# A hybrid decoder layer on one core: the second token half of x loaded transposed, its root spread by one product, and other PSUM banks for early turns

## The chip, the cores and the metric

The kernel runs on one core of a Trainium2 chip. The metric is the device time of one execution in microseconds. Before the change it is 1091.62 us, the median of 3 runs (1091.47 to 1091.79).

In the text, TensorE is the matrix engine (PE in the profile; PEld are its weight loads), VectorE is DVE, ScalarE is ACT, GpSimd is POOL, and SyncE (SP) issues most DMAs. "Turn" stands for a transposition on TensorE: a product with the identity matrix, whose result lies in PSUM.

## The reference

x has 1024 tokens (T) of 1024 features (D), in float32. The change lies in the first steps of the layer:

```
mod = silu(c) @ w_ada + b_ada                       # sh1, sc1, g1, sh2, sc2, g2
h = rmsnorm(x, pre_w_mix) * (1 + sc1) + sh1         # rmsnorm: x * rsqrt(mean(x*x) + EPS) * w
proj = h @ w_in                                     # columns: aq, ak, av, hq, hf, hi, hg
attn = sliding-window attention(rope(aq), rope(ak), av), normalised
rec  = gated linear recurrence(hq, hf, hi), normalised, times silu(hg)
x = x + g1 * rmsnorm(concat(attn, rec) @ w_out)
h = rmsnorm(x, pre_w_mlp) * (1 + sc2) + sh2
x = x + g2 * rmsnorm(square(relu(h @ w_up)) @ w_down)
```

Products of the projections and the MLP are made in three parts: each operand is split into a rounded upper part (hi) and a rest (lo), and hi\*hi, hi\*lo and lo\*hi are summed.

## The kernel before

The tokens are two halves (th 0 and 1) of four blocks of 128 (tb 0 to 7), the features eight blocks of 128 (kb 0 to 7). The projection contracts over features, so h is needed with features on the partitions, while x is loaded with tokens on the partitions (`load_x`, line 105; one tile of 128x512 per token block and column half). For each token half the kernel does this:

- `norm_sq` (188) squares the rows of x on ScalarE and sums them (tile jx); `norm_rstd` (199) makes the root of a half, a column of four values for each token partition (VectorE t_x, POOL r_x); `norm_scale` (207) multiplies the rows of x by it.
- `first_T` (215) turns the four 128x128 pieces of one feature block of a token half into one PSUM bank xT.
- `first_evac` (231) makes the block of h from it by `split_evac` (223): ScalarE computes hhi = a\*xT + sh, with a and sh per feature; POOL f = hhi - sh; VectorE hlo = a\*xT - f. hhi and hlo are the two parts of h.
- `first_mm` (394) and `proj3` (510) are the products: pq (queries, 512 columns) and pk (keys and values, 256 columns).

The eight feature blocks of the first half are worked through by a loop (lines 462 to 508): at block kb the engines evacuate xT0 of kb, split the weights of kb+1 (`first_wq` on ScalarE, `first_wql` on VectorE), do the upper parts of the products of the four token blocks (`first_mm` with part 0), turn the next block, and do the lower parts. Into this loop are woven the modulations: `mod_mm` and `mod_fold` at kb 1, and, for the feature blocks 4 to 7, sums over the weight rows on VectorE (`mod_sum`, 309, tile macc) and a turn of the sum at kb 3 and 5 (`mod_turn`, 318, tile pmt). Their results a, sh and ns are what `first_evac` of the next block waits for.

At kb 3 the SP queue gets the loads of x for the second half; at kb 5 and 6 its squares are made, at kb 6 its root, at kb 6 and 7 VectorE scales its rows, and at kb 7 its first two blocks are turned (xT1). Lines 673 to 692 do the rest: `qproj` evacuates pq of the first half, the blocks 2 to 7 of the second half are turned and evacuated, `kvproj` evacuates pk, and the query product of token block 4 (pq4) is done three blocks behind. Then `rope` rotates the queries and keys.

From line 695 on, `filler` gives TensorE work beside attention, in the order of i: queries and keys/values of token blocks 4 to 7 (pq4 pk4 pq5 pk5 ... ), then `values`. The first attention block begins with i = 4, by turning the queries (tile pqT).

What sets the order: the engine handles ACT, DVE, POOL, PE and SP are wrapped by a class `Queue`. Between `pin(True, ...)` (358) and `pin(False, ...)` (693) the instructions of ScalarE, VectorE, POOL and TensorE run in the order of the program text. Outside, the tile framework orders each engine's instructions itself. SP is pinned only for the loads of the second half of x; everything issued later on SP comes behind these.

PSUM has eight banks, in three pools: `pmm` two (`mm_ps`), `pb` five (`tp_ps`), `pa` one (`a_ps`). In the loop pq0 and pq1 hold the two banks of pmm; pq2, pq3 and the two banks of pk hold four of pb. One bank of pb and the one of pa remain for the turns, and a turn waits until the bank's former content has been read. In SBUF the tiles of `hT_` come from a pool of 32 buffers, those of `m_` from one of 16.

Of the kernel before, what the change touches and what calls it, by code (L numbers as in the profile page):

```python
# [47 lines left out]
def hybrid_layer(ctx: ExitStack, tc: tile.TileContext, I, out, dbg=None):  # L48
# [46 lines left out]
    def a_ps(name):  # L95
        return pa.tile([P, 512], F32, tag="aps", name=name)
# [134 lines left out]
    def first_evac(th, kb, pst):  # L231
        hh[kb][th] = (hT_(f"hhi{kb}_{th}", F32R), hT_(f"hlo{kb}_{th}", F32R))
        c = slice(kb, kb + 1)
        split_evac(pst, a1[:, c], sh1[:, c], ns1[:, c], *hh[kb][th], f"f{th}_{kb}")
# [80 lines left out]
            else:  # L315
                DVE.scalar_tensor_tensor(macc1[q], wt, c, macc1[q], ALU.mult, ALU.add)

    def mod_turn(q):
        pst = a_ps(f"pmt{q[0]}")
        for j in range(4):  # L320
            PE.transpose(pst[:, j * P:(j + 1) * P], macc1[q][:, j * P:(j + 1) * P], ident)
        red = small.tile([P, 4], F32, tag="mred", name=f"mred1_{q[0]}")
        DVE.tensor_reduce(red, pst.rearrange("p (j k) -> p j k", j=4), AX.X, ALU.add)
        c = slice(2 * q[0], 2 * q[0] + 2)
        s2 = small.tile([P, 2], F32, tag="m1s", name=f"m1s{q[0]}")
        DVE.tensor_tensor(s2, red[:, 2:4], bT[:, 8 + c.start:8 + c.stop], ALU.add)
        DVE.tensor_tensor(sh1[:, c], red[:, 0:2], bT[:, c], ALU.add)
        DVE.scalar_tensor_tensor(a1[:, c], s2, 1.0, prew1s[:, c], ALU.add, ALU.mult)
        DVE.tensor_scalar(ns1[:, c], sh1[:, c], -1.0, None, ALU.mult)
# [129 lines left out]
        first_mm(0, tb, 1)  # L459

    nextq = {1: (1, 0)}
    for kb in range(1, KB):
        q = nextq.get(kb)
        first_evac(0, kb, xT0[kb])
        if kb + 1 < KB:
            first_wq(kb + 1)
        if kb == 3:
            norm_scale(0, 1, ACT)
            pin(True, SP)
            for hf in range(2):  # L470
                for tb in range(4, TB):
                    load_x(tb, (hf,))
            pin(False, SP)
        if kb == 3:
            mod_sum((2, 0), (7,))
        if kb in (3, 5):
            first_wql(kb + 1)
        for tb in range(3):
            first_mm(kb, tb, 0)
        if q:  # L480
            mod_mm(q)
            mod_copy(q)
        if kb in (3, 5):
            mod_turn((kb // 2 + 1, 0))
        first_mm(kb, 3, 0)
        if kb not in (3, 5) and kb + 1 < KB:
            first_wql(kb + 1)
        if q:
            mod_fold(q)
        if kb in (1, 3, 5):  # L490
            first_kv((kb + 1) // 2, DVE)
        if kb < 5:
            mod_sum(*{1: ((2, 0), (0, 4, 1)), 2: ((2, 0), (5, 2, 6, 3)),
                      3: ((3, 0), (0, 4, 1)), 4: ((3, 0), (5, 2, 6, 3, 7))}[kb])
        if kb + 1 < KB:
            xT0.append(first_T(0, kb + 1, a_ps if kb in (2, 4, 6) else tp_ps))
        if kb in (5, 6):
            for tb in range(4, TB):
                norm_sq(tb, (kb - 5,))
        if kb == 6:  # L500
            norm_rstd(1, 0, 4)
            norm_scale(1, 0, DVE)
        if kb == 7:
            norm_scale(1, 1, DVE)
        if kb == KB - 1:
            xT1 = [first_T(1, 0), first_T(1, 1, a_ps)]
        for tb in range(4):
            first_mm(kb, tb, 1)

# [17 lines left out]
    sinT = cload("sinT", [P, TB, 16], pool=XA)  # L527

    def qproj(tb):
        if tb < 5:  # L530
            pq = pq0[tb]
        else:
            pq = mm_ps(f"pq{tb}")
            proj3(pq, htok(tb), wq)
        q = m_(f"q{tb}")
        if tb in (0, 1):
            DVE.tensor_scalar(q, pq, 0.125, None, ALU.mult)
        else:
            ACT.activation(q, pq, AF.Copy, scale=0.125)
        qn.append(q)  # L540

    def kvproj(tb):
        if tb < 4:
            pk = pk0[tb]
        else:
            pk = mm_ps(f"pk{tb}")
            proj3(pk[:, :256], htok(tb), wkv)
        kv = XA.tile([P, 256], F32, tag="kv", bufs=8, name=f"kv{tb}")
        if tb < 4:
            DVE.tensor_copy(kv, pk[:, :256])  # L550
        else:
            ACT.activation(kv, pk[:, :256], AF.Copy)
        kvn.append(kv)

    def rope(tb, nh, eng=POOL):
# [115 lines left out]
            next(att[tb])  # L671

    att = [attention(tb) for tb in range(TB)]
    for kb in range(2):
        qproj(kb)
        first_evac(1, kb, xT1[kb])
    pq0.append(mm_ps("pq4"))
    for kb in range(2, KB + 3):
        if kb < KB:
            first_evac(1, kb, first_T(1, kb, mm_ps if kb == 2 else tp_ps))  # L680
        if kb == 2:
            qproj(2)
            qproj(3)
        if kb == KB:
            for tb in range(4):
                kvproj(tb)
        if kb > 2:
            proj3(pq0[4], htok(4)[kb - 3:kb - 2], wq[kb - 3:kb - 2], kb == 3, kb == KB + 2)
    for tb in range(4):
        eng = DVE if tb < 2 else POOL  # L690
        rope(tb, 8, eng)
# [1046 lines left out]
def layout(x, c, w_ada, b_ada, pre_w_mix, w_in, attn_sinks, attn_out_w, lb_table,  # L1738
           hg_norm_w, w_out, post_w_mix, pre_w_mlp, w_up, w_down, post_w_mlp):
    A = {}  # L1740
    f = lambda a: np.ascontiguousarray(a)
    cols = lambda v: f(np.asarray(v).reshape(-1, P).T)
    A["x"] = f(np.asarray(x)[0])
    t_cT = cols(np.asarray(c)[0])
    wa = np.asarray(w_ada)[0]
    w1 = wa[:, :2048]
    A["wada1"] = f(w1.reshape(4, 2, P, 2, 4, 256).transpose(3, 4, 0, 2, 1, 5).reshape(2, 4, 4, P, 512))
    A["wada1"][:, 2:] = (w1.reshape(2, 4, P, 2, 4, 256)[:, :, :, :, 2:].transpose(0, 4, 1, 2, 3, 5)
                         .reshape(2, 2, 4, P, 512))
    A["wada1"][:, 0] = (w1.reshape(2, 2, 2, P, 2, 8, P)[:, :, :, :, :, :2].transpose(1, 5, 0, 3, 4, 2, 6)  # L1750
                        .reshape(2, 4, P, 512))
    A["wada"] = f(wa.reshape(KB, P, 6, 2, 512).transpose(2, 3, 0, 1, 4))
    ba = np.asarray(b_ada)[0]
    t_bT = cols(ba)
    A["b_g1"] = f(ba[2048:3072])
    A["b_g2"] = f(ba[5120:6144])
    t_prew1 = cols(np.asarray(pre_w_mix)[0])
    t_prew2 = cols(np.asarray(pre_w_mlp)[0])
    A["postw1"] = f(np.asarray(post_w_mix)[0])
    A["postw2"] = f(np.asarray(post_w_mlp)[0])  # L1760
    wi = np.asarray(w_in)[0]
    perm = [0, 4, 1, 5, 2, 6, 3, 7]
    A["w_q"] = f(wi[:, :512].reshape(D, 8, 64)[:, perm].reshape(KB, P, 512))
    A["w_kv"] = f(wi[:, 512:768].reshape(4, 2, P, 256).transpose(0, 2, 1, 3).reshape(4, P, 512))
    A["w_hv"] = f(wi[:, 1792:2304].reshape(KB, P, 512))
    hd = np.stack([wi[:, 1280:1792], wi[:, 768:1280], wi[:, 2304:2816]])
    A["w_hd"] = f(hd.reshape(3, KB, P, 4, P).transpose(3, 0, 2, 1, 4).reshape(4, 3, P, D))
    sk = np.asarray(attn_sinks)[0]
    order = [0, 1, 4, 5, 2, 3, 6, 7]
    A["sinks"] = f(np.broadcast_to(sk[order], (P, 8)))  # L1770
    A["attw"] = f(np.asarray(attn_out_w)[0].reshape(8, 64)[perm].reshape(4, P).T)
    A["lbt"] = f(np.asarray(lb_table).reshape(2, 4, P).transpose(2, 0, 1))
    A["hgw"] = f(np.asarray(hg_norm_w)[0].reshape(P, 1))
    wo = np.asarray(w_out)[0]
    A["w_o"] = f(np.concatenate([wo[:512].reshape(8, 64, D)[perm].reshape(4, P, D), wo[512:].reshape(4, P, D)]))
    A["w_u"] = f(np.asarray(w_up)[0].reshape(KB, P, 32, P).transpose(2, 1, 0, 3).reshape(32, P, D))
    A["w_dn"] = f(np.asarray(w_down)[0].reshape(32, P, D))
    A["tab"] = f(np.concatenate([np.eye(P, dtype=np.float32), t_cT, t_bT, t_prew1, t_prew2], 1))
    inv = (np.float64(500000.0) ** (-np.arange(0, 16, 2) / 16.0)).astype(np.float32)
    ang = (np.arange(1024, dtype=np.float32)[:, None] * inv[None, :]).astype(np.float64)  # L1780
    co, si = np.cos(ang).astype(np.float32), np.sin(ang).astype(np.float32)
    A["cosT"] = f(np.concatenate([co, co], 1).reshape(TB, P, 16).transpose(1, 0, 2))
    A["sinT"] = f(np.concatenate([-si, si], 1).reshape(TB, P, 16).transpose(1, 0, 2))
    i = np.arange(P)
    A["mle"] = (i[None, :] <= i[:, None]).astype(np.int32)
    A["fle"] = (i[:, None] <= i[None, :]).astype(np.float32)
    si_, ti = i[:, None], i[None, :]
    A["hmask"] = (si_ <= ti).astype(np.int32)
    A["rmask"] = f(np.broadcast_to((np.arange(512) % CH != 0).astype(np.float32), (P, 512)))
    return A  # L1790
# [14 lines left out]
```

## Time and profile before

The profiled execution took 1092.06 us by the clock of the runs, its span from the first to the last instruction is 1090.1 us.

| what | number |
|---|---|
| median of 3 runs | 1091.62 us |
| profiled execution, its span | 1092.06 us, 1090.1 us |
| TensorE busy | 1072.2 us, 98% of the span |
| VectorE, ScalarE, POOL busy | 803.5, 585.2, 374.5 us |
| HBM read, written | 147.51, 55.05 MB |
| granted TensorE clock | 0.997 |

How to read it: a row of the timeline gives start, duration, engine, operation, the tile written, the tiles read, the shape and a count where several instructions are merged; in square brackets stand the idle time of the engine ahead of it and what ended it. A matmul row `128*128 128x512` is a product with a 128x128 stationary and a 128x512 moving operand; products overlap, so the distance between two starts is the time that one takes from the queue, and the duration is longer. Two instructions stand for one product in plain fp32. A row of the stretches gives from:to, its length, the busy time and number of instructions of the engine, the granted clock, the share of the DMA engines and GB/s. A row of the waits gives who waited for whom: us in total, times, the longest. A row of the groups ends with the busy time and the mean duration in ns, then the idle time ahead of the group and who ended it; a row of a tile gives minimum, median and maximum ns. Line numbers in the rows are mostly 39, the line of the wrapper.

### The profile page before, as it was taken

Reading aid. Unit: us, or ns where it says so; the run is one execution under the profiler, and the core shown is the slowest. Engines: PE = TensorE matmul, PEld = TensorE weight load, DVE = VectorE, ACT = ScalarE, POOL = GpSimd, SP = SyncE. Lnnn points to the kernel's source line nnn. Section 1 sums busy time; section 2 is a strip of 40 time slices with the busy share of each in tenths; the row PEclk is TensorE's granted clock in tenths of the full one; section 3 lists DMA queues with packets and bytes.
Section 4 is the critical chain, followed back from the end, with each engine's and each line's share of the span. In section 5 each row is a group of like instructions: output and inputs, shape, how many; then the busy total and the mean of one; then the engine's idle time right before and its main releaser. Section 6 shows DMA issues by size and latency. Waiting matters only on the chain.

```text
span 1090.1 us, 16105 instructions
## 1 busy us (share of the span) xinstructions
PE 1072.2 (98%) x5479; PEld 875.2 (80%) x5479; DVE 803.5 (74%) x1336; ACT 585.2 (54%) x1207; POOL 374.5 (34%) x497
## 2 busy tenths in 40 slices
PE   8999999999999999999999999999999999999996
PEld 6888666788888888888888888888888888888885
DVE  4867768878865564559766767777778788899886
ACT  4535553454554754566655555556575543446435
POOL 1163211143234653432543433344333333320014
PEclk9999999999999999999999999999999999999998
DMA  9702202544310252324577776767999888998638
GB/s 355 268 20 65 91 1 59 167 128 126 115 59 30 88 192 88 135 84 140 187 248 251 230 249 217 242 234 248 296 358 323 270 299 264 327 309 276 198 97 139
DMA packets 101826, 203.63 MB, mean 187 GB/s; under 512 B 13040, under 2 KB 13808, under 8 KB 101744
## 3 DMA queue, kind: packets, MB, share of 16 engines
q1 hardware_dynamic: 86256, 155.04, 42.1%
q0 software_dynamic: 15200, 47.20, 14.7%
q8 instruction: 43, 0.70, 0.3%
q10 hardware_dynamic: 288, 0.36, 0.1%
q14 instruction: 39, 0.32, 0.1%
HBM read 147.51 MB, written 55.05 MB: 186 GB/s over the span
## 4 chain that ended last, share of the span: by engine, by line
PE 87%; DMA 4%; DVE 4%; ACT 2%; POOL 1%; issue 1%; SPq 0%; DVEq 0%; POOLq 0%; ACTq 0%
PE pda L39 16%; PE pua L39 14%; PE pdc L39 8%; PE po L39 8%; PE puc L39 7%; PE pu L39 4%; PE pdb L39 4%; PE pub L39 3%; PE phg L39 3%; PE pv L39 3%; PE phq L39 3%; PE phf L39 3%; PE pq L39 2%; DMA wa<-wada 2%; PE o L39 1%; PE sc L39 1%
## 5 line engine op out<-in xcount | busy, mean ns | idle before, releaser
L39 POOL TENSOR_TENSOR b<-b,b 128x512 f32<-128x512 f32 x64 | 90.7, 1417 | 229.8 <-DMA b<-w_dn 229.4
L39 ACT ACTIVATE dw<-dwr 128x512 fp32r<-128x512 f32 x72 | 45.4, 630 | 52.1 <-DMA dwr<-td 36.5
L39 ACT ACTIVATE s<-s 128x512 f32<-128x512 f32 x84 | 53.0, 631 | 32.4 <-DVE s L39 31.1
L39 DVE TENSOR_TENSOR dw<-dwr,dw 128x512 fp32r<-128x512 f32 x72 | 55.6, 773 | 6.4 <-ACT dw L39 6.3
L39 DVE TENSOR_TENSOR acc<-pda,acc 128x512 f32<-128x512 f32 x68 | 46.7, 686 | 14.0 <-PE pda L39 13.8
L39 POOL DMA_DIRECT2D td<-b x64 | 36.4, 569 | 19.0 <-POOL b L39 19.0
L39 DVE TENSOR_TENSOR wt<-s,wt 128x512 fp32r<-128x512 f32 x42 | 39.4, 939 | 2.6 <-ACT wt L39 2.5
L39 ACT ACTIVATE s<-pua 128x512 f32<-128x512 f32 x28 | 16.7, 597 | 40.5 <-PE pua L39 40.5
L39 POOL TENSOR_TENSOR rrf<-ssf,mhalf 128x1 f32<-128x1 f32 x7 | 7.6, 1080 | 88.0 <-DVE ssf L39 88.0
L39 ACT ACT_TABLE_LOAD x28 | 35.9, 1283 | 1.7 <-PEq L1798 1.2
L39 DVE SCALAR_TENSOR_TENSOR macc<-wada,cs,macc 128x512 f32<-128x512 f32 x42 | 33.7, 803 | 3.6 <-DMA wada<-wada 3.0
L39 POOL DMA_DIRECT2D b<-w_dn x64 | 34.5, 542 | 2.7 <-issue 2.7
L39 POOL TENSOR_TENSOR comb<-comb,rd 128x512 f32<-128x512 f32 x8 | 11.7, 1459 | 63.3 <-DVE rd L39 44.2
L39 PE MATMUL pua<-bt_0h,wt 128*128 128x512 f32 x84 | 32.7, 389 | 0.0
L39 PE MATMUL pua<-bt_1h,wt 128*128 128x512 f32 x84 | 32.7, 389 | 0.0
L39 PE MATMUL pua<-bt_2h,wt 128*128 128x512 f32 x84 | 32.7, 389 | 0.0
L39 PE MATMUL pua<-bt_3h,wt 128*128 128x512 f32 x84 | 32.7, 389 | 0.0
L39 DVE TENSOR_TENSOR wt<-a,wt 128x512 fp32r<-128x512 f32 x42 | 30.7, 732 | 0.9 <-ACT wt L39 0.9
L39 ACT ACTIVATE wt<-s 128x512 fp32r<-128x512 f32 x42 | 26.3, 626 | 8.0 <-DVE s L39 7.8
L39 DVE TENSOR_TENSOR s<-puc,s 128x512 f32<-128x512 f32 x14 | 9.7, 690 | 27.9 <-issue 25.4
L39 DVE TENSOR_TENSOR acc<-pdc,acc 128x512 f32<-128x512 f32 x36 | 24.7, 686 | 6.7 <-PE pdc L39 6.6
L39 PE MATMUL pda<-dw,du_6h 128*128 128x512 f32 x96 | 29.6, 389 | 0.0
(766 smaller groups left out, 3764.8 us busy)
## 6 DMA issues: line engine op xcount, KB each, us to landing
dur<-ud SPq DMA_DIRECT2D x112, 256.0 KB, 4.5
wada<-wada SPq DMA_DIRECT2D x64, 256.0 KB, 3.5
b<-w_dn POOLq DMA_DIRECT2D x64, 256.0 KB, 5.4
td<-b POOLq DMA_DIRECT2D x64, 256.0 KB, 3.4
dwr<-td SPq DMA_DIRECT2D x64, 256.0 KB, 4.9
a<-w_u SPq DMA_DIRECT2D x56, 256.0 KB, 4.5
dwr<-w_dn SPq DMA_DIRECT2D x48, 256.0 KB, 4.3
ud<-s SPq DMA_DIRECT2D x42, 256.0 KB, 3.5
```

Of the source, the lines that this page charges most:

```text
L39: ins = op(*args, **kw)
```

## The change

- The host also lays out the second token half of x transposed (`xT1`, eight blocks of 128x512). At kb 5 and 6 of the loop eight loads bring these into SBUF. The turns of the second half and the scaling of its rows are left out. x itself is still loaded, for its squares.
- The root of the second half is spread over all partitions: `dgx` holds four diagonal matrices with the root's values, and one product with a matrix of ones puts the 512 values on each partition of a bank `rbx`. It stands at the head of kb 7. VectorE multiplies each block of xT1 by rbx in place, the first three at once, the others ahead of the evacuations (at step kb the multiplication of kb+2, then the evacuation of kb+1). `first_evac` then reads SBUF in place of PSUM.
- Of the squares of the second half, six are made at kb 5 and two at kb 6, where they were four and four.
- pq4 and pq5 are done together in the loop over kb, one block behind the evacuation, and pq5 no longer among the fillers.
- `qproj` and `kvproj` of the first half are all on ScalarE; the queries of token blocks 0 and 1 and the four keys/values were on VectorE.
- At kb 3 the last step of `mod_sum` for (2, 0) stands ahead of `first_evac`; `mod_turn` at kb 3 uses a bank of `pb`; the turn of x made at kb 3 uses the bank of `pa`, those at kb 4 and 5 a bank of `pb` (4 was in `pa`). `first_wql` at kb 3 and 5 comes behind `mod_turn`.

```diff
-    def mod_turn(q):
-        pst = a_ps(f"pmt{q[0]}")
+    def mod_turn(q, mk):
+        pst = mk(f"pmt{q[0]}")
...
+    xT1 = []
     for kb in range(1, KB):
         q = nextq.get(kb)
+        if kb == 3:
+            mod_sum((2, 0), (7,))
+        if kb == 7:
+            rbx = tp_ps("rbx")
+            PE.matmul(rbx, lhsT=ones, rhs=dgx.rearrange("p a t -> p (a t)"), start=True, stop=True)
         first_evac(0, kb, xT0[kb])
         if kb + 1 < KB:
             first_wq(kb + 1)
+        else:
+            for j in range(3):
+                DVE.tensor_tensor(xT1[j], xT1[j], rbx, ALU.mult)
+            first_evac(1, 0, xT1[0])
+            first_evac(1, 1, xT1[1])
...
-        if kb == 3:
-            mod_sum((2, 0), (7,))
-        if kb in (3, 5):
-            first_wql(kb + 1)
...
-            mod_turn((kb // 2 + 1, 0))
+            mod_turn((kb // 2 + 1, 0), tp_ps if kb == 3 else a_ps)
         first_mm(kb, 3, 0)
-        if kb not in (3, 5) and kb + 1 < KB:
+        if kb + 1 < KB:
             first_wql(kb + 1)
...
-            xT0.append(first_T(0, kb + 1, a_ps if kb in (2, 4, 6) else tp_ps))
+            xT0.append(first_T(0, kb + 1, a_ps if kb in (2, 3, 6) else tp_ps))
+        for tb, hf in {5: ((4, 0), (5, 0), (6, 0), (7, 0), (4, 1), (5, 1)), 6: ((6, 1), (7, 1))}.get(kb, ()):
+            norm_sq(tb, (hf,))
         if kb in (5, 6):
-            for tb in range(4, TB):
-                norm_sq(tb, (kb - 5,))
+            for j in range(4 * kb - 20, 4 * kb - 16):
+                xT1.append(load_raw(hT_ if j < 6 else m_, f"xT1_{j}", I["xT1"][j]))
         if kb == 6:
             norm_rstd(1, 0, 4)
-            norm_scale(1, 0, DVE)
-        if kb == 7:
-            norm_scale(1, 1, DVE)
-        if kb == KB - 1:
-            xT1 = [first_T(1, 0), first_T(1, 1, a_ps)]
+            dgx = t_("dgx", (P, 4, P))
+            DVE.tensor_tensor(dgx, ident.unsqueeze(1).broadcast_to([P, 4, P]),
+                              rx[1].unsqueeze(2).broadcast_to([P, 4, P]), ALU.mult)
...
-    for kb in range(2):
-        qproj(kb)
-        first_evac(1, kb, xT1[kb])
-    pq0.append(mm_ps("pq4"))
-    for kb in range(2, KB + 3):
-        if kb < KB:
-            first_evac(1, kb, first_T(1, kb, mm_ps if kb == 2 else tp_ps))
-        if kb == 2:
-            qproj(2)
-            qproj(3)
-        if kb == KB:
-            for tb in range(4):
-                kvproj(tb)
-        if kb > 2:
-            proj3(pq0[4], htok(4)[kb - 3:kb - 2], wq[kb - 3:kb - 2], kb == 3, kb == KB + 2)
+    pq0.append(a_ps("pq4"))
+    for kb in range(KB):
+        if 0 < kb < KB - 1:
+            if kb + 2 < KB:
+                DVE.tensor_tensor(xT1[kb + 2], xT1[kb + 2], rbx, ALU.mult)
+            first_evac(1, kb + 1, xT1[kb + 1])
+        (qproj if kb < 4 else kvproj)(kb % 4)
+        if kb == 0:
+            pq0.append(mm_ps("pq5"))
+        for tb in (4, 5):
+            proj3(pq0[tb], htok(tb)[kb:kb + 1], wq[kb:kb + 1], kb == 0, kb == KB - 1)
...
+    A["xT1"] = f(np.asarray(x)[0, 512:].T.reshape(KB, P, 512))
```

Beside these, `qproj` takes pq from the list for tb < 6 (it was tb < 5), and the branches to VectorE in `qproj` and `kvproj` are gone.

More of the change, by code (lines that the diff above doesn't have):

```diff
@@ L529, in qproj @@
     def qproj(tb):
-        if tb < 5:
+        if tb < 6:
             pq = pq0[tb]
@@ L535, in qproj @@
         q = m_(f"q{tb}")
[L536 to L539, printed above, removed]
+        ACT.activation(q, pq, AF.Copy, scale=0.125)
         qn.append(q)
@@ L548, in kvproj @@
         kv = XA.tile([P, 256], F32, tag="kv", bufs=8, name=f"kv{tb}")
[L549 to L552, printed above, removed]
+        ACT.activation(kv, pk[:, :256], AF.Copy)
         kvn.append(kv)
```

## The prediction

> **What bounds the kernel now.** I read the page first: TensorE is busy almost throughout, so only what leaves or enters its queue, or stalls it, can move the end.
>
> ```profile
> span 1090.1 us, 16105 instructions
> PE 1072.2 (98%) x5479; PEld 875.2 (80%) x5479; DVE 803.5 (74%) x1336; ACT 585.2 (54%) x1207; POOL 374.5 (34%) x497
> ```
>
> Then the waits of TensorE, first from 20 to 80 us, where the change lies (its two largest), then from 80 us to the end (seven rows, 3.7 us in sum; the first and the last stand here):
>
> ```profile
> PE pmt L39 <- DVE hlo L39: 1.0, 1, 1.0
> PE pmt L39 <- DVE macc L39: 0.9, 1, 0.9
> ...
> PE rb L39 <- DVE dg L39: 1.6, 4, 0.6
> ...
> PE phg L39 <- ACT f L39: 0.2, 1, 0.2
> ```
>
> Next, TensorE alone by stretches: the upper parts of k block 7 (53.95), their lower parts with the first two second-half turns, the stage with the other six turns and pq4, and pq5:
>
> ```profile
> 53.95:56.74 2.79, 2.79 (x18) 1.00 0.02 6
> 56.74:59.02 2.28, 2.28 (x19) 1.00 0.00 0
> 59.02:68.64 9.62, 9.01 (x51) 1.00 0.00 0
> 71.51:76.97 5.46, 5.46 (x26) 1.00 0.02 5
> ```
>
> The clock column is 1.00 in all. The third row holds only 24 products, as many as the fourth, and lasts 4.2 us longer: that is the room here. A piece of TensorE's timeline shows what a turn costs:
>
> ```profile
> 61.32 0.60 PE L39 MATMUL xT<-c_tab,x 128*128 128x128 f32 x4
> 61.68 0.48 PE L39 MATMUL pq<-wq1h,hhi 128*128 128x512 f32 x1
> 62.00 0.39 PE L39 MATMUL pq<-wq1l,hhi 128*128 128x512 f32 x1
> ...
> 79.85 0.60 PE L39 MATMUL pqT<-c_tab,q 128*128 128x128 f32 x4
> ```
>
> Four turns hold the queue 0.36 us (61.32 to 61.68), and the product behind them starts its successor 0.32 later, where 0.23 is usual (5.46 / 24): 0.45 a block. The last row, the start of attention, is my mark.
>
> **The turns of the second half go.** Two of eight lie in the 2.28 row, back to back: 2 x 0.36 + 0.09 = 0.81, so that row becomes 1.47. The other six cost 6 x 0.45 = 2.7 of the 9.62; 24 products at 0.23 take 5.52, so 9.62 - 2.7 - 5.52 = 1.4 are stalls. Pq4 and pq5 together become 48 x 0.23 = 11.04, against 9.62 + 5.46 = 15.08. If nothing stalls, this saves 0.81 + 4.04 = 4.85 us. Pk4 and pk5 keep their lengths, and the moved pq5 takes no cover from anything: it stood ahead of the mark.
>
> **The spread of the root is new on TensorE.** One fp32 product of 128x512; a like one stands near the end:
>
> ```profile
> 1079.65 1.02 PE L39 MATMUL pdly<-x,c_tab 128*128 128x512 f32 x2
> ```
>
> It is two instructions, 1.02 us to the modelled end. The tail by which an end outlasts the successor's start is 0.39 - 0.23 = 0.16 in the timeline above, so it holds the queue 0.86, and 0.09 more behind it as a turn does: 0.95 us. The low bound is 0.36, a set of turns, the high one 1.11, without the tail. It is all on the path: k block 7's products stand behind it in TensorE's queue, also while it waits for dgx.
>
> **The early turns get other banks.** These rows are the two stalls:
>
> ```profile
> 33.12 0.75 DVE L39 SCALAR_TENSOR_TENSOR macc<-wa,cs,macc 128x512 f32<-128x512 f32 x1
> 34.45 0.74 DVE L39 SCALAR_TENSOR_TENSOR macc<-wa,cs,macc 128x512 f32<-128x512 f32 x1
> 35.34 0.63 PE L39 MATMUL pmt<-c_tab,macc 128*128 128x128 f32 x4 [0.91 <-DVE macc L39]
> 37.07 0.69 DVE L39 TENSOR_TENSOR wkv2l<-wkvr,wkv2h 128x512 fp32r<-128x512 f32 x1
> 38.35 0.40 PE L39 MATMUL pq<-wq4h,hhi 128*128 128x512 f32 x1
> ...
> 44.78 0.75 DVE L39 SCALAR_TENSOR_TENSOR macc<-wa,cs,macc 128x512 f32<-128x512 f32 x1
> 45.45 0.75 DVE L39 SCALAR_TENSOR_TENSOR hlo<-xT,a,f 128x512 fp32r<-128x512 f32 x1
> 46.25 0.66 PE L39 MATMUL pmt<-c_tab,macc 128*128 128x128 f32 x4 [1.00 <-DVE hlo L39]
> ```
>
> In block 3 the last sum now precedes hlo: behind the sum at 33.12 it ends at 33.12 + 2 x 0.75 and a gap, about 34.65, and the turn follows 0.15 later as before (34.45 + 0.74 to 35.34), at 34.80 for 35.34. In block 5 hlo's bank is no longer waited for, but the sum is, and VectorE's work up to it is the same: 44.78 + 0.75 + 0.15 = 45.68 for 46.25. The second wait swallows the first gain: 0.57 us in all. The lower weight part of block 4, put behind the turn's reduction and its small steps, follows these at 37.07 - 0.54 = 36.53 and ends 0.7 later, at 37.2; its product comes at 38.35 - 0.54 + 0.23 = 38.0: nothing, and VectorE is where it was, at 37.2 for 37.07. In block 5 it is alike. Block 5's turn of x, now in the ordinary bank, waits for hlo, done at 46.2; TensorE comes to it 1.2 us after the other turn, at 46.9: nothing.
>
> **Is dgx in time?** TensorE reaches the spread at 53.95 - 0.57 = 53.38.
>
> ```profile
> L39 ACT ACTIVATE jx<-x x8: 618/622/627, 43.5 to 51.2; 128x512 f32<-128x512 f32 x8
> 51.90 0.17 DVE L39 SCALAR_TENSOR_TENSOR t_x<-ssx 128x4 f32<-128x4 f32 x1 [0.78 <-ACT jx L39]
> 52.15 1.01 POOL L39 TENSOR_TENSOR r_x<-t_x,mhalf 128x4 f32<-128x4 f32 x1 [2.41 <-DVE t_x L39]
> 88.96 0.69 DVE L39 TENSOR_TENSOR comb<-comb,rd 128x512 f32<-128x512 f32 x1
> ```
>
> Two squares move to block 5, which frees 1.2 us ahead of the others, and everything is 0.57 earlier. ScalarE alone would allow t_x at 50.1; VectorE's order (hlo and a lower weight part before it) puts it at about 50.4, an estimate. Then the root ends at 51.7, and dgx, priced by the last row, at 52.4. Cover 1.0 us; beyond that it costs one for one.
>
> **The second half's blocks** now need two passes on VectorE. The durations are those of the groups from 57 to 72 us, the multiplication's is that of a sum of a PSUM and an SBUF tile on the page:
>
> ```profile
> L39 ACT ACTIVATE hhi<-xT,sh,a 128x512 fp32r<-128x512 f32 x8 | 5.9, 779 | 6.4 <-PE xT L39 6.4
> L39 DVE SCALAR_TENSOR_TENSOR hlo<-xT,a,f 128x512 fp32r<-128x512 f32 x8 | 5.8, 749 | 3.1 <-POOL f L39 3.1
> L39 POOL TENSOR_SCALAR f<-hhi,ns 128x512 f32<-128x512 f32 x8 | 5.5, 697 | 7.4 <-ACT hhi L39 7.4
> L39 ACT ACTIVATE q<-pq 128x512 f32<-128x512 f32 x3 | 1.7, 595 | 2.2 <-PE pq L39 2.2
> L39 DVE TENSOR_TENSOR s<-puc,s 128x512 f32<-128x512 f32 x14 | 9.7, 690 | 27.9 <-issue 25.4
> ```
>
> A block costs VectorE 0.69 + 0.75 = 1.44, ScalarE 0.78 + 0.60 = 1.38 with the evacuation moved to it, POOL 0.70, and TensorE consumes one in 6 x 0.23 = 1.38. The chain multiplication, hhi, f, hlo is 2.92 (some 3.1 with handoffs), and as written it laps over two blocks (a multiplication stands two hlo ahead): 1.54 a block. The multiplication is bounded by the 0.60 of an evacuation and the 0.75 of hlo; 0.69 has its very kinds of operands. For hhi out of SBUF the neighbours are jx at 0.62 and hhi out of PSUM at 0.78; I keep 0.78. Its start: the spread lands at 54.5, three multiplications to 56.6, hlo of block 0 at 57.45, of block 1 at 58.2, of block 7 at 58.2 + 6 x 1.54 = 67.4. TensorE has block 7's products from 54.33 to 58.59 (2.79 + 1.47), needs the first hlo two products later, at 59.05, and the last at 59.05 + 7 x 1.38 = 68.71. So 1.3 us remain, and VectorE's backlog is off the path. The scalings and evacuations taken from VectorE lay beside TensorE's work and give nothing.
>
> **The eight added loads** (2 MB) follow x in SP's queue:
>
> ```profile
> 34.63 4.69 SPq L39 DMA_DIRECT2D x<-x  x8
> x<-x SPq DMA_DIRECT2D x16, 256.0 KB, 5.0
> ```
>
> Issued at 0.59 each from about 40, or from 45.6 where a buffer is freed by the last sum, they land from 50.6 at the latest for the first and 54.8 for the last; block 0 is wanted at 54.5, block 7 at about 65. Queued behind them are small tables and parts of w_hv, all with readers long after. Nothing; if the first came later than 55.8 (54.5 and the 1.3 us of slack), it would cost one for one.
>
> **The sum.** 4.85 + 0.57 - 0.95 = 4.47 us: attention starts at 75.4. What follows hangs on finished work, not on the clock, and nothing there is changed, so I carry it whole. The profiled execution took 1092.06 us (1.96 beside its span), 0.44 over the median of 1091.62. 1092.06 - 4.47 = 1087.59; less 0.44, **1087.2 us**.
>
> **Rivals.** *B, the blocks pace TensorE.* Hlo's first input moves from PSUM to SBUF, so it reads two SBUF tiles, as macc does. Macc stretches where f runs:
>
> ```profile
> 42.72 0.70 POOL L39 TENSOR_SCALAR f<-hhi,ns 128x512 f32<-128x512 f32 x1 [3.97 <-ACT hhi L39]
> 42.82 1.14 DVE L39 SCALAR_TENSOR_TENSOR macc<-wa,cs,macc 128x512 f32<-128x512 f32 x1
> ```
>
> That is 1.14 against 0.75. If each hlo pays it, a block takes 0.69 + 1.14 = 1.83, block 1's hlo ends 0.4 later than above, and the last at 58.6 + 6 x 1.83 = 69.6, 0.9 late: 1088.1. If each waits a whole f, 0.70 + 0.75 = 1.45, a block takes 2.14 and the last, from 58.9, ends at 58.9 + 12.84 = 71.7, 3.0 late: 1090.2. Against it: f can run under the multiplication, which reads one SBUF tile and one PSUM bank like the present hlo, never stretched. The Trainium skill (SBUF — State Buffer, "Who interferes with whom") says that a VectorE instruction with two SBUF inputs and a GpSimd instruction that reads SBUF exclude each other, the later one blocking until the first is done. By that rule the 2.14 case is the harsh end; the 0.39 of the row agrees in sign and is less than a whole f.
>
> *C, the gain is given back later.* Behind the pinned stretch the tile framework orders instructions anew, by its own estimate of when each is ready. The price is bounded by TensorE's waits behind the mark: doubled, they cost 3.7, 1090.9; halved, they add 1.8. For it: attention's chains (rb on dg) are tight. Against: no load or weight there comes at a fixed time.
>
> *D, slower: a block's four steps do not overlap.* Place: the loop of pq4 and pq5. Price: 3.1 a block, the last hlo at 58.2 + 18.6 = 76.8, 8.1 late: 1087.2 + 8.1 = 1095.3. It eats the gain from 2.5 us a block on, (68.71 + 4.47 - 58.2) / 6. Against: in the groups above eight blocks pass within the 15 us of that view, under 1.9 each, though one block's steps take longer, and the multiplications run ahead.
>
> **How the numbers follow.** The forecast has 0.72, B 0.13, C 0.10, D 0.05. This kernel's measurement can tell about 0.2%, 2.2 us, from no change. Faster: 0.72 and 0.08 of B, 0.80. Same: the rest of B, and C, 0.15. Slower: D, 0.05. The range goes up to 1090.2, the harsh end of B; down to 1085.0: the spread at its low bound (0.59 less) and C the other way round, 1.8 less, make 1084.8. It leaves out C's upper end, D and a corner of the forecast, under 0.2.
>
> **What would show it.** Right: no turns after k block 7, pmt at about 34.8 and 45.7, the spread at 53.4 without a wait and 0.86 long, pq4 and pq5 alternating without gaps from 58.6 to 69.6, attention's first turn at 75.4, the rest shifted alike. Wrong: a wait of the spread for dgx, of pq for hlo or hhi, hlo well above 0.75, or a smaller shift at the end than at the mark.

## The result, and the profile after

The changed kernel takes 1086.6 us (median of 6 runs, 1086.37 to 1087.54) beside 1091.7 us for the kernel before in the same session (1091.39 to 1092.88): ratio 0.9953, 95% interval 0.9942 to 0.9964. It is faster by about 5 us, clear of the interval; 1087.2 was predicted, 1085.0 to 1090.2. The profiled execution took 1086.42 us, 5.64 less than that of before. The head of its page:

```profile
span 1084.6 us, 16059 instructions
PE 1067.8 (98%) x5449; PEld 872.2 (80%) x5449; DVE 798.8 (74%) x1331; ACT 587.6 (54%) x1213; POOL 371.3 (34%) x497
```

TensorE is as full as it was, with 30 instructions and 4.4 us of busy time less. Its waits from 20 to 80 us are now one row; the two sums of that row are what is left of the early turns' stalls:

```profile
PE pmt L39 <- DVE macc L39: 1.3, 2, 1.0
```

TensorE's timeline (start, duration, what, idle time ahead of it) at the places that the prediction named. The first row, block 2's first product, is a point ahead of every edit:

```profile
27.02 0.40 PE L39 MATMUL pq<-wq2h,hhi 128*128 128x512 f32 x1
...
34.30 0.63 PE L39 MATMUL pmt<-c_tab,macc 128*128 128x128 f32 x4 [0.37 <-DVE macc L39]
...
45.19 0.63 PE L39 MATMUL pmt<-c_tab,macc 128*128 128x128 f32 x4 [0.97 <-DVE macc L39]
...
52.85 1.02 PE L39 MATMUL rbx<-dgx,ones 128*128 128x512 f32 x2
...
53.94 0.39 PE L39 MATMUL pq<-wq7l,hhi 128*128 128x512 f32 x1
...
67.94 0.39 PE L39 MATMUL pq<-wq7h,hlo 128*128 128x512 f32 x1
...
74.60 0.60 PE L39 MATMUL pqT<-c_tab,q 128*128 128x128 f32 x4
```

The mark, attention's first turn, went from 79.85 to 74.60: 5.25 us. But the same point ahead of the edits lay elsewhere in the kernel before, and the reason is at the very start, where nothing was edited: there a product that reads x waits for the load of x. First the rows of before, then those of after:

```profile
1.66 4.71 PE L39 MATMUL spare<-spare,ones_r 128*128 128x512 f32 x11 [1.66 <-DVE spare L121]
6.98 0.49 PE L39 MATMUL spare<-x,ones 128*128 128x128 f32 x2 [0.61 <-DMA x<-x]
...
27.52 0.39 PE L39 MATMUL pq<-wq2h,hhi 128*128 128x512 f32 x1
```

```profile
1.65 4.09 PE L39 MATMUL spare<-spare,ones_r 128*128 128x512 f32 x11 [1.65 <-DVE spare L121]
6.46 0.49 PE L39 MATMUL spare<-x,ones 128*128 128x128 f32 x2 [0.71 <-DMA x<-x]
```

The product that reads x started 0.52 us earlier in this execution, and 0.50 us of that were still there at block 2. The eleven spare products ahead of it also took 0.62 us less, but that is not the reason: with the turns kept (below) they took 4.23 us, the product behind them still waited 1.72 us for x, to 7.61, and block 2 began at 28.16. In all fourteen profiles block 2 begins 20.5 to 20.8 us behind the product that reads x; in the twelve experiments this is at 27.15 to 28.24. It is a property of the execution, so I count every mark from its own block 2: 52.33 us before, 47.58 after, **4.75 us gained** where 4.47 was predicted. The stretches (from:to, length, busy time, clock, share of DMA, GB/s) say where. First those of before that the prediction does not show: all of k block 7, then pk4, then pk5:

```profile
53.95:59.02 5.07, 5.07 (x35) 1.00 0.01 3
...
68.64:71.51 2.87, 2.87 (x26) 1.00 0.00 0
...
76.97:79.85 2.88, 2.88 (x26) 1.00 0.29 60
```

Then those of after: the spread with all of k block 7, pq4 and pq5 together, pk4 with pk5:

```profile
52.85:57.90 5.05, 5.05 (x28) 1.00 0.11 41
57.90:68.84 10.94, 10.94 (x50) 1.00 0.00 0
68.84:74.60 5.76, 5.76 (x50) 1.00 0.00 0
```

Up to k block 7, 0.60 us came from the early turns (53.95 - 27.52 against 52.85 - 27.02). In k block 7 the spread took what its two turns gave (5.07, 5.05). The stage with the turns and pq4 and that of pq5 (9.62 + 5.46 = 15.08 before) gave 15.08 - 10.94 = 4.14, and pk4 and pk5 nothing (5.75, 5.76).

Behind the mark nothing was given back: mark to end of span is 1010.25 before and 1010.00 after. TensorE's waits from 80 us on still sum to 3.7 us; the first and the last row:

```profile
PE rb L39 <- DVE dg L39: 1.6, 4, 0.6
...
PE x2T L39 <- DVE h L39: 0.2, 1, 0.2
```

The blocks of the second half, on VectorE: the matrix for the spread, the first three multiplications, and the evacuations of blocks 1 and 7.

```profile
51.37 0.69 DVE L39 TENSOR_TENSOR dgx<-c_tab,r_x 128x512 f32<-128x512 f32 x1 [1.12 <-POOL r_x L39]
53.91 1.88 DVE L39 TENSOR_TENSOR xT<-xT,rbx 128x512 f32<-128x512 f32 x3
...
57.56 0.75 DVE L39 SCALAR_TENSOR_TENSOR hlo<-xT,a,f 128x512 fp32r<-128x512 f32 x1 [0.52 <-POOL f L39]
...
66.80 0.75 DVE L39 SCALAR_TENSOR_TENSOR hlo<-xT,a,f 128x512 fp32r<-128x512 f32 x1 [0.82 <-POOL f L39]
```

From 57.56 to 66.80 six blocks pass, (66.80 - 57.56) / 6 = 1.54 each, the predicted pace. The evacuation at 66.80 ends at 67.55 and its product runs at 67.94: 0.39 us to spare, not the 1.3 predicted. Rows of the tiles f and hlo (minimum, median, maximum ns), and of the groups the one of hhi; the nine are the eight blocks of the second half and, ahead of them, block 7 of the first:

```profile
L39 POOL TENSOR_SCALAR f<-hhi,ns x9: 692/694/1207, 52.5 to 66.1; 128x512 f32<-128x512 f32 x9
L39 DVE SCALAR_TENSOR_TENSOR hlo<-xT,a,f x9: 750/752/769, 53.2 to 66.8; 128x512 fp32r<-128x512 f32 x9
```

```profile
L39 ACT ACTIVATE hhi<-xT,sh,a 128x512 fp32r<-128x512 f32 x9 | 7.2, 810 | 6.0 <-DVE xT L39 3.9 <-PE xT L39 2.1
```

Hlo, whose inputs both lie in SBUF now, takes 0.75 to 0.77 us at every block. One f of the nine was stretched, to 1.21 us. It is the second of this pair on POOL, from 56.32 to 57.53, and so starts beside the first hlo, which runs from 56.27 to 57.04; the hlo of block 1 (57.56, above) waited 0.52 us for it.

```profile
55.55 1.98 POOL L39 TENSOR_SCALAR f<-hhi,ns 128x512 f32<-128x512 f32 x2 [2.34 <-ACT hhi L39]
```

### The profile page after: what moved, and what is told of

It reads as the page before. It is cut to its first block, busy times and chain, and to the rows that moved or that the text cites. A ratio compares the mean times of both kernels' runs of the same rounds, so it can differ in the third digit from the quotient of the medians.

```text
span 1084.6 us, 16059 instructions
## 1 busy us (share of the span) xinstructions
PE 1067.8 (98%) x5449; PEld 872.2 (80%) x5449; DVE 798.8 (74%) x1331; ACT 587.6 (54%) x1213; POOL 371.3 (34%) x497
## 3 DMA queue, kind: packets, MB, share of 16 engines
q0 software_dynamic: 15200, 47.20, 14.4%
## 4 chain that ended last, share of the span: by engine, by line
PE 89%; DVE 4%; DMA 4%; ACT 1%; issue 1%; POOL 1%; SPq 0%; DVEq 0%; ACTq 0%; POOLq 0%
PE pda L39 16%; PE pua L39 14%; PE pdc L39 8%; PE po L39 8%; PE puc L39 7%; PE pu L39 4%; PE pdb L39 4%; PE phg L39 4%; PE pub L39 4%; PE phf L39 3%; PE pv L39 3%; PE phq L39 3%; PE pq L39 3%; DMA wa<-wada 2%; PE o L39 1%; PE pk L39 1%
## 5 line engine op out<-in xcount | busy, mean ns | idle before, releaser
L39 POOL TENSOR_TENSOR b<-b,b 128x512 f32<-128x512 f32 x64 | 87.4, 1365 | 223.4 <-DMA b<-w_dn 223.0
L39 DVE TENSOR_TENSOR wt<-s,wt 128x512 fp32r<-128x512 f32 x42 | 36.1, 859 | 2.6 <-ACT wt L39 2.5
L39 DVE TENSOR_TENSOR wt<-a,wt 128x512 fp32r<-128x512 f32 x42 | 34.5, 823 | 0.9 <-ACT wt L39 0.9
L39 PE MATMUL pda<-dw,du_7h 128*128 128x512 f32 x96 | 29.6, 389 | 0.0
L39 PE MATMUL pdc<-dw,du_3h 128*128 128x512 f32 x96 | 29.6, 389 | 0.0
```

The costliest lines, as they stand in the source:

```text
L39: ins = op(*args, **kw)
```

## The experiments

Starts and marks from TensorE's timeline of each profile; "gain" is the time from block 2 to the mark against the kernel before (52.33). Each ratio is to the kernel before on the same chip (medians 1091.7 to 1092.3 us).

| kernel | median us | ratio, interval | block 2 | mark | between | gain | mark to end |
|---|---|---|---|---|---|---|---|
| before | 1091.7 | | 27.52 | 79.85 | 52.33 | | 1010.25 |
| after | 1086.6 | 0.9953 (0.9942 to 0.9964) | 27.02 | 74.60 | 47.58 | 4.75 | 1010.00 |
| banks only | 1091.47 | 0.9994 (0.9985 to 1.0002) | 27.95 | 79.67 | 51.72 | 0.61 | 1009.83 |
| no other banks | 1087.37 | 0.9960 (0.9946 to 0.9973) | 27.42 | 75.52 | 48.10 | 4.23 | 1009.78 |
| lead lost | 1096.43 | 1.0038 (1.0025 to 1.0051) | 28.24 | 84.80 | 56.56 | -4.23 | 1010.60 |
| turns kept | 1091.53 | 0.9994 (0.9985 to 1.0002) | 28.16 | 79.80 | 51.64 | 0.69 | 1010.30 |
| two spreads | 1088.44 | 0.9968 (0.9956 to 0.9981) | 27.55 | 75.98 | 48.43 | 3.90 | 1011.12 |
| three spreads | 1089.53 | 0.9974 (0.9965 to 0.9983) | 27.66 | 76.98 | 49.32 | 3.01 | 1010.62 |
| squares late | 1091.08 | 0.9988 (0.9979 to 0.9997) | 27.56 | 79.33 | 51.77 | 0.56 | 1010.07 |
| late but busy | 1090.37 | 0.9982 (0.9973 to 0.9991) | 27.15 | 77.53 | 50.38 | 1.95 | 1010.27 |
| squares 4 and 4 | 1087.27 | 0.9956 (0.9943 to 0.9969) | 27.75 | 75.51 | 47.76 | 4.57 | 1009.79 |
| turn later | 1087.42 | 0.9961 (0.9948 to 0.9974) | 28.07 | 75.62 | 47.55 | 4.78 | 1009.98 |
| POOL split | 1086.53 | 0.9947 (0.9935 to 0.9960) | 27.75 | 74.95 | 47.20 | 5.13 | 1009.75 |
| combined | 1086.73 | 0.9951 (0.9938 to 0.9965) | 27.80 | 74.77 | 46.97 | 5.36 | 1009.83 |

My theory is the prediction's: the gain is the second half's turns and the stalls they brought, plus the early banks, less the spread. Its rivals are that the blocks pace TensorE, and that the gain is lost or made behind the mark.

**The banks by themselves, and everything but the banks.** The kernel before with the four edits of k blocks 3 to 5; the changed kernel with these four undone.

```diff
-        pst = a_ps(f"pmt{q[0]}")
+        pst = mk(f"pmt{q[0]}")
...
+        if kb == 3:
+            mod_sum((2, 0), (7,))
         first_evac(0, kb, xT0[kb])
...
-            xT0.append(first_T(0, kb + 1, a_ps if kb in (2, 4, 6) else tp_ps))
+            xT0.append(first_T(0, kb + 1, a_ps if kb in (2, 3, 6) else tp_ps))
```

> The kernel before with the early banks alone: the last sum of block 3 ahead of the evacuation, the other banks of the turns, the lower weight parts behind the turn. Theory (TensorE's queue): the two waits of the modulation turns shrink to about 0.4 and 1.0 us, and since the second is set by VectorE's sums the gain is 0.55 us and not the sum of both: 0.5 to 0.6 us under before, about 1091.1. Rival (each stall counts by itself): 1.9 us under before, 1089.8. Rival (the turns have cover elsewhere): no change.

> The kernel after with the early banks undone. Theory: 0.55 us over after, about 1087.2, and the modulation turns wait 0.9 and 1.0 us as before. Rival (each stall counts): 1.9 over after, 1088.5. Rival (cover elsewhere): as after.

The mark moved by 0.61 us with the banks alone, and without them the changed kernel gained 0.52 less. The two parts add up: 0.61 and 4.23 are 4.84, against 4.75 together. A gain of 0.6 is too small for whole times: with the banks alone the interval includes no change, so this part is shown by the profiles only.

**The multiplications' lead.** In the changed kernel only two blocks are multiplied ahead, and each further one directly before its own evacuation, so that the four steps of a block form one chain.

```diff
-            for j in range(3):
+            for j in range(2):
                 DVE.tensor_tensor(xT1[j], xT1[j], rbx, ALU.mult)
...
-            if kb + 2 < KB:
-                DVE.tensor_tensor(xT1[kb + 2], xT1[kb + 2], rbx, ALU.mult)
+            DVE.tensor_tensor(xT1[kb + 1], xT1[kb + 1], rbx, ALU.mult)
             first_evac(1, kb + 1, xT1[kb + 1])
```

> The kernel after with each multiplication right ahead of its own evacuation from block 2 on (two done at once instead of three). Theory: the four steps of a block then follow one another, 0.67 + 0.78 + 0.91 + 0.72 = 3.08 us from start to start in the profile after; block 1's hlo ends at 58.3, block 7's at 58.3 + 6 x 3.08 = 76.8, where 67.9 is wanted: 8.9 us over after, 1095.5, slower than before, and TensorE waits for hhi and hlo in the stage of pq4 and pq5. Rival (the order of multiplications is a detail, the engines overlap anyhow at about 1.5 us a block): within 0.5 us of after.

The kernel is slower than before. TensorE's waits from 20 to 85 us, and then two of VectorE's evacuations, five blocks apart:

```profile
PE pq L39 <- DVE hlo L39: 4.2, 5, 0.8
PE pq L39 <- ACT hhi L39: 1.5, 5, 0.3
PE pmt L39 <- DVE macc L39: 1.4, 2, 1.0
```

```profile
61.81 0.75 DVE L39 SCALAR_TENSOR_TENSOR hlo<-xT,a,f 128x512 fp32r<-128x512 f32 x1 [1.67 <-POOL f L39]
...
77.22 0.75 DVE L39 SCALAR_TENSOR_TENSOR hlo<-xT,a,f 128x512 fp32r<-128x512 f32 x1 [1.73 <-POOL f L39]
```

A block takes (77.22 - 61.81) / 5 = 3.08 us, and the mark comes 8.98 us later than in the changed kernel. This is the price that rival D had, at its place: the three multiplications ahead of the loop decide the sign of the whole change.

**Pq5 beside pq4, with the turns kept.** The kernel before, with pq5 done in the loop of pq4 (`qproj` takes it from there too).

```diff
-    pq0.append(mm_ps("pq4"))
+    pq0 += [mm_ps("pq4"), a_ps("pq5")]
...
-            proj3(pq0[4], htok(4)[kb - 3:kb - 2], wq[kb - 3:kb - 2], kb == 3, kb == KB + 2)
+            for tb in (4, 5):
+                proj3(pq0[tb], htok(tb)[kb - 3:kb - 2], wq[kb - 3:kb - 2], kb == 3, kb == KB + 2)
```

> The kernel before with pq5 done beside pq4 in the loop over the second half, the turns kept. Theory: six turns of 0.45 stay in the queue and only the stalls of that stage find cover: 11.0 + 2.7 = 13.7 us instead of 9.62 + 5.46 = 15.1, so 1.3 us under before, about 1090.4. Rival (the gain of the change is the evacuations' waits, covered by the second product, and the turns are nearly free): 3.5 to 4.5 us under before, 1087 to 1088.

A miss by half: 0.69 us. The head of that stage on TensorE shows why:

```profile
59.64 0.60 PE L39 MATMUL xT<-c_tab,x 128*128 128x128 f32 x4
60.58 0.63 PE L39 MATMUL xT<-c_tab,x 128*128 128x128 f32 x4 [0.34 <-DVE hlo L39]
61.17 0.47 PE L39 MATMUL pq<-wq0h,hhi 128*128 128x512 f32 x1
```

The second turn starts 0.94 us behind the first instead of 0.36, and a first product follows 0.59 behind that: 0.8 us of the stalls lie ahead of the stage's first product, where no pq5 can cover them. The stage takes 14.40 us here (59.64 to 74.04). So the 4.14 us split into 15.08 - 14.40 = 0.68 for pq5 beside pq4, six turns at the predicted 0.45, 2.7, and some 0.8 of stalls that left only with the turns. The turns' own 2.7 and these 0.8 were not taken out by themselves; that they leave with the turns is read from the two stages.

**The price of the spread.** The product issued two and three times, onto the same bank.

```diff
-            PE.matmul(rbx, lhsT=ones, rhs=dgx.rearrange("p a t -> p (a t)"), start=True, stop=True)
+            for _ in range(2):
+                PE.matmul(rbx, lhsT=ones, rhs=dgx.rearrange("p a t -> p (a t)"), start=True, stop=True)
```

> The kernel after with the spread's product made twice into the same bank; the second writes what the first wrote. Theory: the spread lies whole on TensorE's path, so the second adds its own 0.86 us, and the multiplications behind it start as much later: 0.8 to 0.9 over after. Rival (the spread is hidden in a wait of TensorE for k block 7): no change.

> The spread product is issued three times instead of once. Theory: each added product costs 0.85 us at the mark, and what follows is carried whole: mark 1.7 us later than in the changed kernel, counted from the same start, end 1.7 later, median about 1088.3 to 1088.6. Rival: a later mark costs more behind it, as the run with two spreads seemed to show (0.85 at the mark, 1.6 to 2 at the end): end 3.2 to 4 us later, median 1089.8 to 1090.6, with the time from the mark to the end 1.5 us or more above the changed kernel's 1010.0.

TensorE's timeline of the kernel with two, then of that with three; the second row of each is the second product behind the spread:

```profile
53.37 1.88 PE L39 MATMUL rbx<-dgx,ones 128*128 128x512 f32 x4
...
55.32 0.39 PE L39 MATMUL pq<-wq7l,hhi 128*128 128x512 f32 x1
```

```profile
53.51 2.74 PE L39 MATMUL rbx<-dgx,ones 128*128 128x512 f32 x6
...
56.32 0.40 PE L39 MATMUL pq<-wq7l,hhi 128*128 128x512 f32 x1
```

From the spread to that row it is 1.09, 1.95 and 2.81 us with one, two and three: 0.86 each. (A first product lies in between; its start is drawn into the spread's own span, so the distance to the second is taken.) The marks agree, 0.85 and 1.74 later. But the medians are about 1.8 and 2.9 us above the changed kernel's, more than the marks. In the profiles the excess lies behind the mark, 1.12 us with two and 0.62 with three. It does not grow with the shift, and with three spreads it is less than half of the 1.5 that the rival needed, so the profiles speak against that rival; but the median, 0.9 above the theory's range, lies nearer to the rival's. These medians come from different sessions. Beside the kernel before in the same session, 1091.91 and 1092.3, the two lose 1.6 and 2.3 us of the changed kernel's 5.1, and with intervals of about 1 us to either side this is compatible with the theory's 0.86 and 1.7. With two spreads a part of the excess is a wait that the changed kernel lacks; from 80 us on:

```profile
PE pda L39 <- DVE acc L39: 0.5, 1, 0.5
```

All of TensorE's waits from 80 us on sum to 4.2 us there, to 3.7 in the changed kernel, and to 3.8 with three spreads, where they explain next to nothing. Over all fourteen profiles the time from mark to end lies between 1009.75 and 1011.12 us. The rest of the excess, and whether the spreads bring it, stays open.

**The squares.** All eight at k block 6; then four and four, as before the change; then all late again, with eleven spare products ahead of the spread.

```diff
-        for tb, hf in {5: ((4, 0), (5, 0), (6, 0), (7, 0), (4, 1), (5, 1)), 6: ((6, 1), (7, 1))}.get(kb, ()):
+        for tb, hf in {6: [(tb, hf) for hf in range(2) for tb in range(4, TB)]}.get(kb, ()):
```

> The kernel after with all eight squares of the second half at k block 6. Theory: six squares more stand ahead of the sum, at 0.62 us and less each, so t_x comes at 53.3 instead of 50.1, dgx ends at about 55.2 where TensorE wants it at 52.85: a wait of 2.3 us at the spread, and 2.3 us over after, since TensorE's queue stands behind it in order. Rival (the wait is covered, since the products of k block 7 do not need the spread): within 0.3 us of after.

> The kernel after with four squares at k block 5 and four at 6, as in the kernel before. Theory: t_x moves from 50.1 to about 50.8 and dgx ends at 52.7, just ahead of TensorE at 52.85: no change, the cover of 0.8 us pays for it. Rival (the moved squares are part of the gain): 0.6 to 1.2 us over after.

Four and four cost 0.18 us at the mark: dgx is ready just as TensorE arrives, so moving two squares bought cover and almost no time. All late, the wait was as expected and the mark moved by nearly twice as much, 4.19 us. TensorE's timeline, and its stretches: the wait, the spread, the first and the later products of k block 7, pq4 with pq5, pk4 with pk5 (the fifth number is the granted clock):

```profile
55.93 1.25 PE L39 MATMUL rbx<-dgx,ones 128*128 128x512 f32 x2 [2.38 <-DVE dgx L39]
...
57.40 0.63 PE L39 MATMUL pq<-wq7l,hhi 128*128 128x512 f32 x1
```

```profile
53.55:55.93 2.38, 0.00 (x0) 1.00 0.34 129
55.93:57.40 1.47, 1.47 (x4) 0.78 0.00 0
57.40:59.96 2.56, 2.56 (x9) 0.50 0.00 0
59.96:62.63 2.67, 2.67 (x16) 0.96 0.02 6
62.63:73.57 10.94, 10.94 (x50) 1.00 0.00 0
73.57:79.33 5.76, 5.76 (x50) 1.00 0.00 0
```

Behind a pause of 2.38 us the granted clock is 0.50. The three stretches with less than 1.00 stand for 0.22/0.5 x 1.47 + 2.56 + 0.04/0.5 x 2.67 = 3.4 us at half the clock, which is 1.7 us lost, and the stretch from spread to mark takes 23.40 us instead of 21.75 in the changed kernel. The last two stretches are exactly its own. To tell this from ScalarE's and VectorE's late work, the pause was filled:

```diff
+            for _ in range(11):
+                PE.matmul(rbx, lhsT=ones_r, rhs=wq[0][0], start=True, stop=True)
             PE.matmul(rbx, lhsT=ones, rhs=dgx.rearrange("p a t -> p (a t)"), start=True, stop=True)
```

> As the run with all squares at k block 6, where the spread waited 2.38 us and the mark came 4.19 us after the changed kernel's; ahead of the spread eleven products of 128x512 whose result is overwritten keep TensorE busy while it waits (11 x 0.23 = 2.5 us). In that run the profile shows TensorE's granted clock at 0.50 for 2.6 us behind the wait, and the stretch from the spread to the mark at 23.40 us instead of 21.75. Theory: the 1.65 us are the clock that fell in the pause; with the pause filled the clock stays at 1.00, the stretch is 21.75 again, and the mark is 2.5 to 2.8 us after the changed kernel's, counted from the same start: median about 1089.3 to 1089.8. Rival: the 1.65 us are ScalarE's and VectorE's work that came late; then the stretch stays at 23.4 and the mark 4.2 to 4.4 us late, median 1091.1 to 1091.5.

```profile
53.23 2.66 PE L39 MATMUL rbx<-wq0h,ones_r 128*128 128x512 f32 x11
55.73 1.06 PE L39 MATMUL rbx<-dgx,ones 128*128 128x512 f32 x2
...
77.53 0.60 PE L39 MATMUL pqT<-c_tab,q 128*128 128x128 f32 x4
```

With TensorE kept busy the same late spread reaches the mark in 21.80 us at a clock of 1.00, and the mark is 2.80 us late instead of 4.19, at the edge of what the theory gave (0.24 of it arose already at the second early turn, which waited 1.21 us here); the rival falls. The median, 1090.37, is above the range I gave for it and only 0.7 below that of the unfilled run, and the two intervals overlap. The single executions say why: of the eleven with all squares late, three took 1089.30 to 1089.73 us at a mean clock of 0.997 to 0.998, the other eight 1090.50 to 1092.12 at 0.996, and all eleven of the filled kernel had 0.997 to 0.998. So the same pause seems to have lowered the clock in eight executions and not in three; the profile is of one of the eight, so the clock in the three is inferred from their times.

**What is left at the early turns.** Three tries to take the remaining waits for the sums: both turns one token block later; the lower keys/values weights of k block 3 on POOL instead of VectorE; both, with the squares five and three.

```diff
-            mod_turn((kb // 2 + 1, 0), tp_ps if kb == 3 else a_ps)
         first_mm(kb, 3, 0)
+            mod_turn((kb // 2 + 1, 0), tp_ps if kb == 3 else a_ps)
...
-            first_kv((kb + 1) // 2, DVE)
+            first_kv((kb + 1) // 2, POOL if kb == 3 else DVE)
```

> The kernel after with the modulation turns of blocks 3 and 5 behind the fourth token block's upper part instead of ahead of it. Theory: the turn of block 5 is bound by VectorE's last sum and starts when it did; 0.7 us of products move into its wait; the next bound, the evacuation of block 6 that needs the turned sums, takes back a half: 0.35 us under after. Rival (the wait of 1.0 us is all TensorE's loss): 0.7 to 1.0 us under after. Rival (a later turn delays the next block): slower by up to 0.4 us.

> The lower weight part of the keys/values at k block 3 is made by POOL instead of VectorE. In the changed kernel this VectorE step (0.69 us) lies between the two turned sums, and the last sum of block 5 is waited for 0.97 us. Theory: VectorE reaches the last sum about 0.6 us earlier, the turn of block 5 follows at about 0.5 before its place in the changed kernel (45.19, counted from the same start of the products of block 2), but hhi of the next block is then bound by ScalarE's squares, so the mark moves by 0.3 us to the front: median ratio to the changed kernel 0.9997. Rival 1: POOL's step, which reads two SBUF tiles, holds up VectorE's sums and hlo for about its length: mark 0.5 to 0.8 us later, turn of block 5 later too. Rival 2: the wait only moves from the sum to hlo of block 5: turn earlier, mark within 0.1.

> The step of POOL as in the run beside it, with the squares five at k block 5 and three at k block 6, and both turned sums behind the products of the fourth token block instead of the third. Theory: with ScalarE's squares no longer late, the whole 0.6 us of the wait for the last sum and some of the wait at block 3 come back: mark 0.6 to 0.75 us before the changed kernel's, counted from the same start, and a median near 1086.0. Rival: as the turn alone gave nothing (its sum comes 0.2 us later), only the POOL step's 0.3 shows, or the step's loss.

The later turn alone gained 0.03 us: the wait ahead of the second turn shrinks from 0.97 to 0.35 us, but the turn, on which the next evacuation hangs, starts 0.2 later (18.39 us behind block 2 instead of 18.17). POOL's step gained 0.38, as its theory said, although it takes 1.28 us there for 0.69 on VectorE; its second turn and that step:

```profile
45.55 0.63 PE L39 MATMUL pmt<-c_tab,macc 128*128 128x128 f32 x4 [0.59 <-DVE macc L39]
```

```profile
35.53 1.28 POOL L39 TENSOR_TENSOR wkv2l<-wkvr,wkv2h 128x512 fp32r<-128x512 f32 x1 [2.77 <-ACT wkv2h L39]
```

All together gained 0.61 at the mark. The medians, 1086.53 and 1086.73 us beside 1086.6, cannot tell either from the changed kernel, and the expected 1086.0 was not reached: by the profiles these versions are a little better, by the medians that is not shown.

## Why the prediction was right

**The turns of the second half.** Predicted 4.85 us, measured 0.88 + 4.14 = 5.02: k block 7 gave 5.07 - (5.05 - 0.86) = 0.88 for its two turns (0.81 predicted), and pq4 with pq5 took 10.94 us for a predicted 11.04. Nothing stalls in that stage. The split of the 1.4 us of stalls is finer than I had it, as the run with the turns kept shows: part lay ahead of the first product.

**The spread.** It holds the queue 0.86 us, measured three times over. The 0.09 that I added behind it, as behind a turn, is not there, and there was no wait. Dgx ended at 51.37 + 0.69 = 52.06 for a TensorE that came at 52.85: cover 0.8 us for a predicted 1.0. In the run with all squares late that cover was gone, and a wait of 2.38 us cost 4.19 at the mark, not "one for one": the clock fell.

**The early banks.** Predicted 0.57, measured 0.60 in the changed kernel and 0.61 alone. Counted from block 2, the two turns moved by 0.54 and 0.56, and the second wait did swallow the first gain.

**The blocks' pace.** 1.54 us a block, as worked out. The slack is the term that was mis-sized: 1.3 us predicted, 0.39 there. Less the 0.50 of the start, the last product should have come at 68.21 and the last hlo ended at 66.9; they came at 67.94 and 67.55. TensorE was 0.27 early by its own gains, and the blocks 0.65 late. They were so from the second block on: hlo of block 1 should have ended at 57.7 and ended at 57.56 + 0.75 = 58.31, and most of that is its wait of 0.52 for the stretched f. So the change stood nearer to rival B than I thought.

**Rival B, contention.** The cost fell on the other engine. The Trainium skill (SBUF — State Buffer, "Who interferes with whom") has the later of two such instructions blocked until the first is done. The trace agrees on who pays, the f that started just behind an hlo, and not quite on the amount: 0.51 us more, where the rest of that hlo would be 0.7. In blocks 2 to 6 f ran beside a multiplication and stayed at 0.69 to 0.70, the reason the prediction gave against B.

**Rival C** did not happen: the time behind the mark is 0.25 us shorter. Its bound was of the right kind, since among all runs that time varies by 1.4 us. **Rival D** is true of a kernel without the lead, at 3.08 us a block for a predicted 3.1, and a mark 8.98 us later for a predicted 8.1.

**The loads** were misplaced in the account and it did not matter. SP's queue:

```profile
45.17 3.76 SPq L39 DMA_DIRECT2D xT<-xT  x8
```

They stand behind small tables and two loads of w_hv, not ahead of these, and are issued at about the later of the two times that I gave, 45.6. No multiplication waited for one.

**The squares** I had at nothing: undoing that edit costs 0.18 us at the mark.

**From mark to time.** The profiles differ by 5.64 us: 4.75 by the change, 0.50 by the start, 0.25 behind the mark, and the rest beside the span. The medians differ by about 5.1; the 0.35 beyond 4.75 is well within the interval of some 1.2 us to either side, so it can't be told from the scatter. The prediction's 4.47 was 0.28 short: 0.17 in the turns, 0.09 in the spread, 0.03 in the banks.

## What to carry to other kernels

When a stage of the bounding engine holds more time than its instructions need, count the instructions at their usual distance and call the rest stalls; that sum held here to 0.1 us. If data are given in the layout that is wanted, the work saved on one engine comes back as steps on others, and whether those steps are issued a block or two ahead decides the sign (3.08 against 1.54 us a block here). Measure a small edit from a point just ahead of it to a point just behind it: kernels with the same beginning were up to 1.2 us apart at block 2 (27.02 to 28.24).

## What the runs showed of the hardware that was not expected

- In the profiled execution a pause of TensorE of 2.38 us ahead of the spread was followed by a granted clock of 0.50, by the sum above for 3.4 us, worth 1.65 us beyond the pause; eleven spare products in the pause took all but 0.05 of that away. By time and mean clock, three of eleven executions with that pause seem to have kept the clock. Waits of up to 1.2 us at the early turns, and ten of up to 0.8 us in the run without the lead, left the clock at 1.00. The Trainium skill (TensorE: Matmul & The Clock Gate, "Part 1: The HAM clock gate (the "warmup" mystery)") has the clock at half after an idle window of about 3.4 us; here 2.38 us of idle were enough in the profiled execution.
- Eleven spare products at the very start took 4.09 us in one execution and 4.71 in another, and up to 5.06 in other kernels with the same start. What follows did not go by them: the product behind that reads x started at 6.46 to 7.69 us, in twelve of the fourteen profiles when its load released it.
- An fp32 product of 128x512 holds TensorE's queue 0.86 us, 3.7 times the 0.23 of the split operands' products, and adds nothing to the product behind it.
- ScalarE took 0.80 to 0.82 us for hhi out of SBUF, a little more than the 0.78 out of PSUM that I had kept.
